# Preparing the state-space tables of a hybrid decoder trunk: real and imaginary parts in one operation, B for two units at once

## The chip, the core and the metric

The kernel runs on one core of a Trainium2 chip. Its time is the device time of one execution in microseconds (us). An execution with the profiler on gives the trace. In the trace PE is the matrix engine (PEld its weight loads), DVE the vector engine, ACT the scalar engine, POOL the GpSimd engine, and SP the engine that issues most DMAs; ACT issues some too. Every engine works through its own list of instructions in order and waits at the first one whose inputs are missing.

## What is computed

Two layers over 16 learned and 512 input positions (528 rows, width 1024). Each layer normalises, projects, runs latent attention (4 heads) and a diagonal state-space mixer (32 groups of 16 channels, 64 complex states each) side by side, adds both, and runs a gated feed-forward of width 2816. The part that matters here is the state-space mixer:

```python
lr = min(a_re, -1e-4); li = a_im; dt = exp(log_dt)[:, None]
mag = exp(lr * dt)
lam_re, lam_im = mag * cos(li * dt), mag * sin(li * dt)
den = lr * lr + li * li
coef_re = ((lam_re - 1) * lr + lam_im * li) / den        # complex (lam - 1) / (lr + i li)
coef_im = (lam_im * lr - (lam_re - 1) * li) / den
bbar_re = coef_re * b_re - coef_im * b_im                # per group, state and channel
bbar_im = coef_re * b_im + coef_im * b_re
# s[t] = lam * s[t-1] + bbar u[t];  y[t] = re(c s[t]) + d * u[t]
```

The kernel runs the recurrence in chunks of 8 positions, and for that prepares matrices from the parameters: powers 0 to 8 of `lam`, rotations of the unit-size `lam` in two tables of six (`lo`, `hi`) whose products give all chunk positions, and per unit of 4 groups the products of these powers with B and C.

## The kernel before, in words

A layer's preparation has a common part, `prep_small` (L389 to L564), on arrays of 128 states by 32 groups: two exponentials (`exp`, L403), sine and cosine, the powers `pw` of `lam` (`cmul`, L466), the coefficients `cc` (L482 to L502), the copies `pf` and `pw` in falling order with signs on ACT (L506 to L510), and the tables `el` and `eh` (`lo`, `hi`, L532 to L562). All of its arithmetic is on DVE (`ON["small"]`), nearly all on 32 elements per partition, real and imaginary parts in separate instructions. Four quarters follow. A quarter builds a table for its 8 groups (`prep_tables`, L566: `tab`, a single buffer, sent to a DRAM tile by SP) and handles two units (`prep_mats`, L597). A unit loads its B and C (`bc`, two buffers, DMA issued by ACT, L602), forms `bbar` in six operations on 64 elements (L609 to L612), `X` on DVE or POOL, transposes `X` on PE into `pt` (L631), copies it by ACT into `Xt` (L633), forms `C` on POOL (L637), multiplies `bbar` with it on PE into `pk` (L643) and copies that by ACT into `K` (L651). `pt`, `pk` and the state-space products share one PSUM buffer (`"one"`).

In layer 0 this runs beside the first projection and attention; `prep_mats` there has its six `bbar` operations on DVE and `C` on POOL. For layer 1 it runs in layer 0's feed-forward phases (`step(nxt, 2, ...)`, L1272), with `bbar`, `X`, `C` and the tables on POOL and `prep_small` again on DVE, between the evacuations of the gate and up products (`g`, `hid`) and the low parts of the weights (`wlo`, L254).

The order on each engine comes from a scheduler that plays the program through with its own durations, with priorities; layer 0's preparation has a raised one (`LATER`). So an edit in `prep_small` can move instructions of anything that runs near it, on any engine. Three points that the change can touch:

- The norm's factor of layer 0 (`factor`, L342): PE sums squares into `nacc` (L352), DVE makes the reciprocal root `nw` in a dozen small instructions (L332 to L336), PE spreads it over rows (`nrb`, L371). Products of the first projection go on without it, but PE works in order and stops at `nrb`.
- Buffers of 128 by 2 by 528 values, `pair` (15 of them): the layer's normalised inputs `x` take eight in layer 0, with half of each unused, since that layer multiplies in plain float32.
- The end of the state-space part: the last unit's `ya` (L760, L761), its store and reload (`yd`, `y`), the gelu `u` on ACT and DVE (L773 to L777), and the gated product (`acc<-u`, the glu) that needs all four `u`.

Of the kernel before, what the change touches and what calls it, by code (L numbers as in the profile page):

```python
# [10 lines left out]
F32 = mybir.dt.float32  # L11
# [15 lines left out]
HC = 16  # L27
# [21 lines left out]
BUFS = (2,4,0,2,1)  # L49
V0 = (1,1)  # L50
# [51 lines left out]
def trunk(ctx: ExitStack, tc: tile.TileContext, A, out, dbg=None):  # L102
# [283 lines left out]
    def small(name):  # L386
        return prep_tile("small", NL, 24, name)

    def prep_small(l):  # L389
# [6 lines left out]
        def rnd(o, x, c):  # L396
            E.tensor_scalar(out=o, in0=x, scalar1=c, scalar2=MAGIC, op0=ALU.mult, op1=ALU.add)
            E.tensor_scalar(out=o, in0=o, scalar1=-MAGIC, scalar2=None, op0=ALU.add)
# [4 lines left out]
        def exp(o, x):  # L403
            n, r, s = small("n"), small("r"), small("s")
            xc = small("xc")
            E.tensor_scalar(out=xc, in0=x, scalar1=-87.0, scalar2=88.0, op0=ALU.max, op1=ALU.min)
            rnd(n, xc, 1.4426950408889634)
            stt(r, n, -0.693359375, xc, ALU.mult, ALU.add)
            stt(r, n, 2.12194440e-4, r, ALU.mult, ALU.add)
            E.tensor_scalar(out=s, in0=r, scalar1=1.0 / 5040, scalar2=None, op0=ALU.mult)  # L410
            for c in (1.0 / 720, 1.0 / 120, 1.0 / 24, 1.0 / 6, 0.5, 1.0):
                stt(s, s, c, r, ALU.add, ALU.mult)
            e = prep_tile("int", NL, 2, "e", I32)
            E.tensor_scalar(out=n, in0=n, scalar1=127.0, scalar2=None, op0=ALU.add)
            V.tensor_copy(e, n)
            V.tensor_single_scalar(out=e, in_=e, scalar=23, op=ALU.logical_shift_left)
            stt(o, s, 1.0, e.bitcast(F32), ALU.add, ALU.mult)
# [8 lines left out]
        k, r, z, s, c = (small(n) for n in ("k", "r", "z", "s", "c"))  # L426
# [21 lines left out]
        cs, sn, t = small("cs"), small("sn"), small("t")  # L448
# [9 lines left out]
        pr, pi = (x.rearrange("p (t g) -> p t g", t=9) for x in (pw[:, 0:9 * NL], pw[:, 9 * NL:18 * NL]))  # L458
        E.memset(pr[:, 0], 1.0)
        E.memset(pi[:, 0], 0.0)  # L460
        mul(E, pr[:, 1], mag, cs)
        mul(E, pi[:, 1], mag, sn)
        tq = prep_tile("tq", 4 * NL, 1)
        tq = tq.rearrange("p (t g) -> p t g", t=4)

        def cmul(re, im, d, n, a0, br, bi):  # L466
            br, bi = (x.unsqueeze(1).to_broadcast([128, n, NL]) for x in (br, bi))
            t1 = tq[:, 0:n]
            dr, di, ar, ai = re[:, d:d + n], im[:, d:d + n], re[:, a0:a0 + n], im[:, a0:a0 + n]
            mul(E, dr, ar, br)  # L470
            mul(E, t1, ai, bi)
            tt(E, dr, dr, t1, ALU.subtract)
            mul(E, di, ar, bi)
            mul(E, t1, ai, br)
            tt(E, di, di, t1, ALU.add)

        cmul(pr, pi, 2, 1, 1, pr[:, 1], pi[:, 1])
        cmul(pr, pi, 3, 2, 1, pr[:, 2], pi[:, 2])
        cmul(pr, pi, 5, 4, 1, pr[:, 4], pi[:, 4])
        yield  # L480

        nr, den, u = small("nr"), small("den"), small("u")  # L482
        CR, CI = small("CR"), small("CI")
        ni = pi[:, 1]
        E.tensor_scalar(out=nr, in0=pr[:, 1], scalar1=-1.0, scalar2=None, op0=ALU.add)
# [4 lines left out]
        mul(E, CR, nr, lr)  # L490
        mul(E, u, ni, li)
        tt(E, CR, CR, u, ALU.add)
        mul(E, CR, CR, den)
        mul(E, CI, ni, lr)
        mul(E, u, nr, li)
        tt(E, CI, CI, u, ALU.subtract)
        mul(E, CI, CI, den)
        cc = prep_tile("cc", 3 * NL, 1)
        CRk, CIn, CIp = (cc[:, i * NL:(i + 1) * NL] for i in range(3))
        V.tensor_copy(CRk, CR)  # L500
        E.tensor_scalar(out=CIn, in0=CI, scalar1=sneg, scalar2=None, op0=ALU.mult)
        E.tensor_scalar(out=CIp, in0=CI, scalar1=spos, scalar2=None, op0=ALU.mult)  # L502
# [15 lines left out]
        def square(dr, di, ar, ai):  # L518
            q = small("q")
            mul(E, q, ai, ai)  # L520
            mul(E, dr, ar, ar)
            tt(E, dr, dr, q, ALU.subtract)
            stt(di, ar, 2.0, ai, ALU.mult, ALU.mult)

        def power2(a, n):
            for i in range(n):
                b2 = small("e0"), small("e1")
                square(*b2, *a)
                a = b2
            return a  # L530

        lo_ = prep_tile("el", 2 * LOW * NL, 1)  # L532
        hi_ = prep_tile("eh", 2 * HIGH * NL, 1)
        lo, hi = ([x.rearrange("p (r t g) -> p r t g", r=2, g=NL)[:, r] for r in range(2)] for x in (lo_, hi_))
        a = power2((cs, sn), 3)
        E.tensor_scalar(out=a[1], in0=a[1], scalar1=sneg, scalar2=None, op0=ALU.mult)
        for x, n in ((lo, LOW), (hi, HIGH)):
            E.memset(x[0][:, 0], 1.0)
            E.memset(x[1][:, 0], 0.0)
            w = 1  # L540
            while w < n:
                if w > 1:
                    a = power2(a, 1)
                V.tensor_copy(x[0][:, w], a[0])
                V.tensor_copy(x[1][:, w], a[1])
                k = min(w, n - w) - 1
                if k:
                    cmul(x[0], x[1], w + 1, k, 1, *a)
                w *= 2
            if x is lo:  # L550

                a = small("e0"), small("e1")
                t = small("q")
                (r2, i2), (r4, i4) = ((x[0][:, w], x[1][:, w]) for w in (2, 4))
                mul(E, a[0], r2, r4)
                mul(E, t, i2, i4)
                tt(E, a[0], a[0], t, ALU.subtract)
                t = small("q")
                mul(E, a[1], r2, i4)
                mul(E, t, i2, r4)  # L560
                tt(E, a[1], a[1], t, ALU.add)
            yield  # L562
        prm["mag8", l] = mag8
# [32 lines left out]

    def prep_mats(l, u, ea, eb):  # L597
# [3 lines left out]
        raw = prep_tile("bc", 448, BUFS[0])  # L601
        nc.scalar.dma_start(raw[:, 0:256], A["ssmbc"][l, u])  # L602
        b1, b2, c1, c2 = (raw[:, i * 64:(i + 1) * 64].rearrange("p (g h) -> p g h", g=4) for i in range(4))

        def bh(ap):
            return ap[:, gs].unsqueeze(2).to_broadcast([128, 4, HC])

        bb1, bb2, t = (raw[:, i * 64:(i + 1) * 64].rearrange("p (g h) -> p g h", g=4) for i in (4, 5, 6))
        for o, x, y, ci in ((bb1, b1, b2, "CIn"), (bb2, b2, b1, "CIp")):  # L609
            mul(ea, o, x, bh(prm["CR"]))  # L610
            mul(ea, t, y, bh(prm[ci]))
            tt(ea, o, o, t, ALU.add)  # L612
# [63 lines left out]
    class Normed:  # L676
# [757 lines left out]
```

## Time and profile before

| | |
|---|---|
| median of 3 runs | 1327.66 us (1321.62 to 1329.62) |
| the profiled execution | 1326.85 us, its span 1325.1 us |
| PE busy | 1273.1 us, 96% of the span |
| DVE, ACT, POOL busy | 793.2, 433.8, 379.2 us |
| layer 0 up to its feed-forward | 0 to some 305 us |
| layer 0's feed-forward, with layer 1's preparation | to some 707 us |

The page of the profile gives busy times, a chain of waits that ended last, and groups of instructions. [...] Instructions of short length overlap in the timeline, so the step from one start to the next says what one costs its engine. A float32 product of 264 columns is one instruction in the program's order and two on PE in the trace.

### The profile page before, as it was taken

Reading aid. Unit: us, or ns where it says so; the run is one execution under the profiler, and the core shown is the slowest. Engines: PE = TensorE matmul, PEld = TensorE weight load, DVE = VectorE, ACT = ScalarE, POOL = GpSimd, SP = SyncE. Lnnn points to the kernel's source line nnn. Section 1 sums busy time; section 2 is a strip of 40 time slices with the busy share of each in tenths; the row PEclk is TensorE's granted clock in tenths of the full one; section 3 lists DMA queues with packets and bytes.
Section 4 is the critical chain, followed back from the end, with each engine's and each line's share of the span. In section 5 each row is a group of like instructions: output and inputs, shape, how many; then the busy total and the mean of one; then the engine's idle time right before and its main releaser. Section 6 shows DMA issues by size and latency. Waiting matters only on the chain.

```text
span 1325.1 us, 20705 instructions
## 1 busy us (share of the span) xinstructions
PE 1273.1 (96%) x8242; PEld 1146.9 (87%) x8242; DVE 793.2 (60%) x1539; ACT 433.8 (33%) x725; POOL 379.2 (29%) x365
## 2 busy tenths in 40 slices
PE   9888999998999999999999999899999999999996
PEld 7677877998999999999999998789788888888885
DVE  8775673577984556357554279765854445445545
ACT  4211444333332232223233226553422222222231
POOL 3544233551174434025304354356200000000001
PEclk9899998999989999999999999999999999999998
DMA  5467543132234444344434536212233332333321
GB/s 196 148 176 185 137 146 93 57 96 68 93 103 140 112 115 104 105 115 114 110 96 124 180 96 217 64 64 65 80 95 86 106 95 92 86 109 95 93 83 64
DMA packets 83728, 145.94 MB, mean 110 GB/s; under 512 B 23472, under 2 KB 51632, under 8 KB 83632
## 3 DMA queue, kind: packets, MB, share of 16 engines
q1 hardware_dynamic: 80032, 141.32, 36.2%
q10 hardware_dynamic: 3600, 3.30, 0.8%
q8 instruction: 65, 1.06, 0.3%
q14 instruction: 31, 0.25, 0.1%
HBM read 121.17 MB, written 23.43 MB: 109 GB/s over the span
## 4 chain that ended last, share of the span: by engine, by line
PE 72%; DVE 9%; ACT 2%; issue 1%; DMA 1%; POOL 1%; DVEq 0%; SPq 0%; ACTq 0%; POOLq 0%
PE da L277 18%; PE ua L277 18%; PE ga L277 17%; PE acc L277 10%; DVE h L197 1%; PE pvo L1103 1%; DVE sq L197 1%; PE acc L265 1%; PE nrb L371 1%; DVE wlo L197 1%; DVE wo L197 1%; PE nacc L352 1%; PE pvo L1106 1%; PE pk L643 1%; DVE x L311 1%
## 5 line engine op out<-in xcount | busy, mean ns | idle before, releaser
L253 ACT CAST whi<-raw 128x1024 fp32r<-128x1024 f32 (+3 forms) x174 | 174.3, 1002 | 536.5 <-issue 145.3
L277 PE MATMUL ga<-x,whi 128*128 128x264 f32 (+1 forms) x1056 | 226.6, 322 | 6.8 <-ACT x L310 4.9
L277 PE MATMUL ua<-x,whi 128*128 128x264 f32 (+1 forms) x1056 | 226.5, 323 | 0.0
L277 PE MATMUL da<-hid,whi 128*128 128x264 f32 (+2 forms) x1088 | 225.3, 316 | 0.3 <-DVE hid L197 0.3
L277 PEld LDWEIGHTS ga<-x,whi 128*128 128x128 f32 x1056 | 163.8, 189 | 25.1 <-ACT x L310 5.6
L197 DVE TENSOR_TENSOR wlo<-raw,whi 128x1024 fp32r<-128x1024 f32 (+1 forms) x130 | 172.3, 1326 | 17.3 <-ACT whi L253 15.1
L277 PEld LDWEIGHTS ua<-x,whi 128*128 128x128 f32 x1056 | 165.9, 191 | 15.9
L277 PEld LDWEIGHTS da<-hid,whi 128*128 128x128 f32 x1088 | 167.3, 188 | 13.9 <-DVE hid L197 0.5
L277 PE MATMUL ua<-x,wlo 128*128 128x264 f32 (+1 forms) x528 | 143.3, 326 | 3.1 <-DVE wlo L197 3.1
L277 PE MATMUL da<-hid,wlo 128*128 128x264 f32 (+2 forms) x544 | 143.7, 317 | 0.3
L277 PE MATMUL ga<-x,wlo 128*128 128x264 f32 (+1 forms) x528 | 142.1, 323 | 0.0
L197 POOL TENSOR_TENSOR wlo<-raw,whi 128x1024 fp32r<-128x1024 f32 (+2 forms) x44 | 95.9, 2180 | 129.6 <-ACT whi L253 129.6
L197 POOL TENSOR_TENSOR o<-h,nr 128x256 f32<-128x256 f32 x8 | 6.1, 797 | 363.8 <-ACT nr L375 363.8
L197 DVE TENSOR_TENSOR h<-da,h 128x528 f32<-128x528 f32 (+2 forms) x50 | 33.9, 677 | 125.8 <-PE da L277 125.8
L277 PEld LDWEIGHTS ua<-x,wlo 128*128 128x128 f32 x528 | 89.1, 191 | 10.7 <-DVE wlo L197 3.3
L277 PEld LDWEIGHTS da<-hid,wlo 128*128 128x128 f32 x544 | 90.2, 188 | 8.6 <-DVE wlo L197 1.3
L197 DVE TENSOR_TENSOR g<-ua,R 128x528 f32<-128x528 f32 (+1 forms) x44 | 30.7, 698 | 110.4 <-PE ua L277 110.3
L277 PEld LDWEIGHTS ga<-x,wlo 128*128 128x128 f32 x528 | 87.9, 189 | 7.7 <-POOL wlo L197 0.4
L265 PE MATMUL acc<-x,raw 128*128 128x264 f32 x320 | 79.5, 408 | 0.0
L197 DVE TENSOR_TENSOR g<-ga,nr 128x528 f32<-128x528 f32 (+1 forms) x44 | 30.7, 698 | 76.7 <-PE ga L277 75.9
L265 PEld LDWEIGHTS acc<-x,raw 128*128 128x128 f32 x320 | 63.8, 203 | 11.9 <-issue 0.5
L197 POOL TENSOR_TENSOR Ct<-bc,pw 128x576 f32<-128x576 f32 x16 | 23.6, 1476 | 112.5 <-PE pk L643 112.5
(291 smaller groups left out, 2182.4 us busy)
## 6 DMA issues: line engine op xcount, KB each, us to landing
raw<-w_gate SPq DMA_DIRECT2D x44, 512.0 KB, 3.6
raw<-w_up SPq DMA_DIRECT2D x44, 512.0 KB, 3.6
raw<-w_down SPq DMA_DIRECT2D x32, 448.0 KB, 3.4
raw<-w_in SPq DMA_DIRECT2D x20, 512.0 KB, 4.2
mat<-mat SPq DMA_DIRECT2D x16, 528.0 KB, 4.1
mt<-k SPq DMA_DIRECT2D x16, 512.0 KB, 4.7
raw<-w_down SPq DMA_DIRECT2D x16, 512.0 KB, 3.5
mat<-tab SPq DMA_DIRECT2D x16, 272.0 KB, 2.7
```

The costliest lines, as they stand in the source:

```text
L197: e.tensor_tensor(out=o, in0=a, in1=b, op=op)
L253: S.copy(hi[:, :n], raw[:, :n])
L265: T.matmul(acc[:, a, 0:hw], w[0][:, off + k * 128:off + (k + 1) * 128], xs[k][:, c0 + a * hw:c0 + (a + 1) * hw], start=k == 0, stop=k == n ...
L277: T.matmul(acc[:, a, 0:hw], wt[:, c], xs[k][:, xi, c0 + a * hw:c0 + (a + 1) * hw], start=j == 0, stop=j == len(terms) - 1)
L311: V.scalar_tensor_tensor(out=lo, in0=src, scalar=scale, in1=hi.bitcast(F32), op0=ALU.mult, op1=ALU.subtract)
L352: T.matmul(acc[:, i:i + 1], x[:, a:a + 128], ones[:, 0:1], start=x is sqs[0], stop=x is sq)
L371: T.matmul(p[:, a - c0:b - c0], y[0:b - a, j:j + 1].to_broadcast([b - a, 128]), ident[0:b - a, 0:b - a], start=True, stop=True)
L643: T.matmul(pk[0:16, g * 128:(g + 1) * 128], bb1[:, g, :], C[:, g * 144 + 16:g * 144 + 144], start=True, stop=True)
L1103: T.matmul(acc[:, a, 0:w], vs[hd // 2, j][0:sn, hd % 2 * 128:hd % 2 * 128 + 128], PT[j][0:sn, 0, c:c + w].bitcast(F32), start=j == 0, stop ...
L1106: T.matmul(acc[:, a, 0:w], vs[hd // 2, j][0:sn, vi, hd % 2 * 128:hd % 2 * 128 + 128], PT[j][0:sn, pi, c:c + w], start=j == 0 and z == 0, s ...
```

## The change

In `prep_small` the real and imaginary parts lie side by side (`two`): a complex product is now two double-width multiplications, the second with the halves read in swapped order, and two half-width additions. The exponential loses two instructions, and the coefficients two. On ACT the eighteen copies in falling order become two that read with a negative step. `prep_inputs` loads B and C of two units at a time, each load as four pieces of 64 values per partition, and forms both units' `bbar` in six operations of 128 elements. In layer 0 these inputs lie in `pair` buffers; the layer's `x` now lie two to a `pair`, which frees four.

```diff
+BCU = 2
-        return prep_tile("small", NL, 24, name)
+        return prep_tile("small", NL, 16, name)
+    def two(name):
+        return prep_tile("two", 2 * NL, 10, name).rearrange("p (r g) -> p r g", r=2)
+    def swapped(x):
+        steps, last = [list(d) for d in x.ap], x[:, 1]
+        steps[1][0] *= -1
+        return bass.AP(last.tensor, last.offset, steps)
...
-            rnd(n, xc, 1.4426950408889634)
+            e = small("e")
+            rnd(n, xc, 1.4426950408889634, MAGIC + 127.0, e)
...
-            E.tensor_scalar(out=n, in0=n, scalar1=127.0, scalar2=None, op0=ALU.add)
-            V.tensor_copy(e, n)
...
-        mul(E, cs, am, c)
-        mul(E, t, b, s)
-        tt(E, cs, cs, t, ALU.subtract)
-        mul(E, sn, am, s)
-        mul(E, t, b, c)
-        tt(E, sn, sn, t, ALU.add)
+        def product2(o, x, re, im, t):
+            n = x.shape[2:-1]
+            mul(E, o, x, both(re, *n))
+            mul(E, t, swapped(x), both(im, *n))
+            tt(E, o[:, 0], o[:, 0], t[:, 0], ALU.subtract)
+            tt(E, o[:, 1], o[:, 1], t[:, 1], ALU.add)
+        lam = two("lam")
+        product2(lam, csn, am, b, two("t"))
...
-        for j in range(9):
-            S.copy(prr[:, j], pr[:, 8 - j])
-            S.activation(pir[:, j], pi[:, 8 - j], AF.Copy, scale=sneg)
+        S.copy(prr, falling(pr))
+        S.activation(pir, falling(pi), AF.Copy, scale=sneg)
...
+    def prep_inputs(l, u, ea):
+        n = BCU * 4
+        if l == 0:
+            raw = pair("bc").rearrange("p a b -> p (a b)")[:, 0:7 * n * HC].bitcast(F32)
+        else:
+            raw = prep_tile("bc", 7 * n * HC, BUFS[0])
+        for i in range(BCU):
+            nc.scalar.dma_start(raw[:, 0:4 * n * HC].rearrange("p (k u x) -> p k u x", k=4, u=BCU)[:, :, i],
+                                A["ssmbc"][l, u + i].rearrange("p (k x) -> p k x", k=4))
...
+        if u % BCU == 0:
+            prep_inputs(l, u, ea)
+        bb1, bb2, c1, c2 = (x[:, u % BCU * 4:u % BCU * 4 + 4] for x in prm["bc"])
...
-                x = pair("x")[:, 0].bitcast(F32)
+                if k % 2 == 0:
+                    self.two = pair("x")
+                x = self.two[:, k % 2].bitcast(F32)
```

DVE has 1542 instructions in the program before and 1440 with the change, ACT 716 and 684, POOL 371 and 347; PE and SP issue as many as before. `prep_small` has, per layer and without what stands between, 173 instructions on DVE before and 134 now, on 6304 and 6144 elements per partition. The order moves on every engine; three places follow.

PE, layer 0's first projection (`acc<-x`), around the factor of the norm. Before:

```order
L265 MATMUL acc<-x,raw 128x264 x48
L352 MATMUL nacc<-cst,sq 128x1 x10
L265 MATMUL acc<-x,raw 128x264 x9
L631 MATMUL pt<-cst,X 128x128 x4
L265 MATMUL acc<-x,raw 128x264 x11
L643 MATMUL pk<-C,bc 16x128 x4
L371 MATMUL nrb<-cst,nw 128x16
```

With the change:

```order
L266 MATMUL acc<-x,raw 128x264 x48
L353 MATMUL nacc<-cst,sq 128x1 x10
L266 MATMUL acc<-x,raw 128x264 x13
L632 MATMUL pt<-cst,X 128x128 x4
L266 MATMUL acc<-x,raw 128x264 x11
L654 MATMUL pk<-C,bc 16x128 x4
L372 MATMUL nrb<-cst,nw 128x16
```

Four more products stand ahead of `nrb`.

ACT, the loads of B and C of the third unit and on (`DMA bc<-ssmbc`), among flips of the tables (`tab<-tab`), copies of `pt` and `pk`, and evacuations of the projection (`cq`, `sq`). Before:

```order
L589 ACTIVATE tab<-tab 128x8x32 [waits DMAHW1_49,DMAHW2_49,DVE_49,Activation_49]
L589 ACTIVATE tab<-tab 128x8x32 [waits DVE_49]
L651 COPY K_644<-pk 16x4x128 [waits DMAHW5_49,DMAHW6_49,DMAHW4_49,DMAHW7_49,PE_49,Pool_49]
L602 DMA bc<-ssmbc 128x256
L589 ACTIVATE tab<-tab 128x8x32 [waits DMAHW0_49,DMAHW7_49,DVE_49,Activation_49]
L589 ACTIVATE tab<-tab 128x8x32 [waits DVE_49]
L633 COPY Xt<-pt 128x512 [waits PE_49]
L651 COPY K_644<-pk 16x4x128 [waits DMAHW3_49,DMAHW4_49,DMAHW2_49,DMAHW5_49,PE_49,Pool_49]
L602 DMA bc<-ssmbc 128x256
```

With the change:

```order
L586 ACTIVATE tab<-tab 128x8x32 [waits DVE_49]
L930 ACTIVATE cq<-acc,gains 128x528 [waits PE_49]
L603 DMA bc<-ssmbc 128x4x64
L603 DMA bc<-ssmbc 128x4x64 [waits DMAHW7_49]
L644 COPY Xt<-pt 128x512 [waits PE_49]
L933 ACTIVATE sq<-acc 128x528
L662 COPY K_575<-pk 16x4x128 [waits DMAHW1_49,DMAHW0_49,DMAHW2_49,PE_49,Pool_49]
L644 COPY Xt<-pt 128x512 [waits DVE_49,PE_49]
```

A load stood behind the copy of a `pk` each time; now both loads of a pair stand ahead of their units' `pt` and `pk`, and all flips of layer 0's four tables stand above this place. The first pair's loads moved the other way: they were ACT's tenth and thirteenth rows, ahead of the first products, and are now behind the flips of `pf` and `pw`.

PE, the end of layer 0's state-space part: the last `ya`, attention's `ptr` and `pvo`, and the glu products `acc<-u`. Before (the first product with the fourth `u`, `u_1857`, stands seven rows below the last one shown):

```order
L761 MATMUL ya<-S,mt 128x66
L1085 MATMUL ptr<-cst,P 128x128 x3
L1103 MATMUL pvo<-PT,v 128x256
L1103 MATMUL pvo<-PT,v 128x272
L1103 MATMUL pvo<-PT,v 128x256 x4
L1085 MATMUL ptr<-cst,P 128x128 x3
L1103 MATMUL pvo<-PT,v 128x256 x2
L265 MATMUL acc<-u_1446,raw 128x264 x2
L265 MATMUL acc<-u_1641,raw 128x264 x2
L265 MATMUL acc<-u_1772,raw 128x264 x2
L1085 MATMUL ptr<-cst,P 128x128
L1103 MATMUL pvo<-PT,v 128x256
```

With the change (the fourth `u` is `u_1759`):

```order
L774 MATMUL ya<-S,mt 128x66
L1116 MATMUL pvo<-PT,v 128x256
L266 MATMUL acc<-u_1674,raw 128x264 x2
L266 MATMUL acc<-u_1348,raw 128x264 x2
L266 MATMUL acc<-u_1543,raw 128x264 x2
L266 MATMUL acc<-u_1674,raw 128x264 x2
L266 MATMUL acc<-u_1348,raw 128x264 x2
L266 MATMUL acc<-u_1543,raw 128x264 x2
L266 MATMUL acc<-u_1674,raw 128x264 x2
L353 MATMUL nacc<-cst,sq 128x1 x5
L266 MATMUL acc<-u_1759,raw 128x264 x6
```

The last `ya` stands later among PE's rows, behind most of attention's work, and the rows left between it and the fourth `u` are fewer.

## Rows read from the trace of the kernel before

**Rows 1.** Busy time by window: engine busy us (instructions), PE's granted clock, DMA share, GB/s.

```profile
350.00:392.00 42.00, 38.93 (x298) 38.71 (x298) 38.44 (x130) 15.11 (x33) 21.41 (x26) 0.92 0.26 77
392.00:707.00 315.00, 314.71 (x2577) 311.05 (x2576) 176.89 (x168) 90.74 (x119) 103.37 (x106) 1.00 0.40 114
```

**Rows 2.** Waits of PE by stretch: who, for whom, us, times, longest.

```profile
PE nrb L371 <- DVE nw L336: 5.6, 1, 5.6
...
PE pk L643 <- ACT Xt L633: 2.3, 1, 2.3
PE nacc L352 <- DVE nr L373: 1.3, 1, 1.3
...
PE acc L265 <- DVE k L197: 1.6, 1, 1.6
...
PE ua L277 <- DVE wlo L197: 3.1, 1, 3.1
```

**Rows 3.** PE alone by window: us, busy, granted clock, DMA share, GB/s.

```profile
48.00:56.00 8.00, 7.23 (x22) 0.58 0.52 166
92.00:96.00 4.00, 4.00 (x13) 0.57 0.38 90
210.00:222.00 12.00, 10.89 (x39) 0.57 0.32 89
```

**Rows 4.** Chain of waits, whole span: start us, us, engine, tile, line, instructions.

```profile
224.10 2.67 PE acc L265 x12
...
338.89 5.86 PE ga L277 x48
...
383.47 8.21 PE ua L277 x44
```

**Rows 5.** Timeline of DVE at the factor: start, us, instruction [idle before <- releaser].

```profile
42.09 0.69 DVE L197 TENSOR_TENSOR X<-bc,pf 128x512 f32<-128x512 f32 x1 [3.77 <-POOL C L197]
...
47.52 1.19 DVE L336 SCALAR_TENSOR_TENSOR nw<-nw 128x5 f32<-128x5 f32 x1
```

**Rows 6.** DMAs issued in 0 to 130 us: KB each, median us to landing.

```profile
mat<-tab SPq DMA_DIRECT2D x8, 272.0 KB, 3.9
...
ud<-u SPq DMA_DIRECT2D x4, 264.0 KB, 5.5
...
bc<-ssmbc ACTq DMA_DIRECT2D x8, 128.0 KB, 4.0
```

**Rows 7.** Waits of DVE, 60 to 130 us.

```profile
DVE bc L197 <- DMA bc<-ssmbc: 13.8, 4, 4.5
DVE tab L197 <- DMA mat<-tab: 4.1, 2, 2.8
```

**Rows 8.** Timeline of DVE in `prep_small`, undisturbed.

```profile
26.54 0.17 DVE L197 TENSOR_TENSOR CI<-CI,den 128x32 f32<-128x32 f32 x1
26.64 0.20 DVE L197 TENSOR_TENSOR bc<-bc,cc 128x64 f32<-128x64 f32 x1
26.78 0.21 DVE L197 TENSOR_TENSOR pw<-pw,tq 128x64 f32<-128x64 f32 x1
```

**Rows 9.** Timeline of DVE late in layer 1's `prep_small`.

```profile
370.09 1.14 DVE L197 TENSOR_TENSOR tq<-el,e 128x32 f32<-128x32 f32 x1
...
376.02 1.45 DVE L197 TENSOR_TENSOR e<-e 128x32 f32<-128x32 f32 x1
...
382.20 1.22 DVE L197 TENSOR_TENSOR wlo<-raw,whi 128x1024 fp32r<-128x1024 f32 x1
```

**Rows 10.** Timeline of ACT: the high part of the same weights.

```profile
373.84 1.05 ACT L253 CAST whi<-raw 128x1024 fp32r<-128x1024 f32 x1 [2.66 <-PE ua L277]
```

**Rows 11.** Timeline of PE: the last of layer 0's `ya`.

```profile
215.84 0.63 PE L761 MATMUL ya<-S,mt 128*128 128x66 f32 x2
```

**Rows 12.** Timeline of DVE: the end of layer 0's last gelu.

```profile
228.25 0.71 DVE L777 SCALAR_TENSOR_TENSOR u<-u,y 128x528 f32<-128x528 f32 x1 [0.71 <-ACT u L776]
```

More of the change, by code (lines that the diff above doesn't have):

```diff
@@ L425, in prep_small @@
         mul(E, th, li, dt)
-        k, r, z, s, c = (small(n) for n in ("k", "r", "z", "s", "c"))
+        k, r, z = (small(n) for n in ("k", "r", "z"))
+        csn = two("csn")
+        c, s = csn[:, 0], csn[:, 1]
         rnd(k, th, 2.0 / math.pi)
@@ L447, in prep_small, with both @@
         E.tensor_scalar(out=am, in0=am, scalar1=-1.0, scalar2=1.0, op0=ALU.mult, op1=ALU.add)
[L448 to L454 removed]
+        def both(ap, *n):
+            return ap.unsqueeze(1).to_broadcast([128, 2, NL]) if not n else ap.unsqueeze(1).unsqueeze(1).to_broadcast([128, 2, *n, NL])
+        def product2(o, x, re, im, t):
[4 more added lines that the diff above has]
+            tt(E, o[:, 1], o[:, 1], t[:, 1], ALU.add)
@@ L480, in prep_small @@
+        cmul(pws, 5, 4, 1, pr[:, 4], pi[:, 4])
         yield
[L482 to L485, printed above, removed]
+        num, den, u, CR = two("num"), small("den"), small("u"), two("CR")
+        E.tensor_scalar(out=num[:, 0], in0=pr[:, 1], scalar1=-1.0, scalar2=None, op0=ALU.add)
+        V.tensor_copy(num[:, 1], pi[:, 1])
         mul(E, den, lr, lr)
@@ L489, in prep_small, with falling @@
         V.reciprocal(out=den, in_=den)
[L490 to L497, printed above, removed]
+        t = two("t")
+        mul(E, CR, num, both(lr))
+        mul(E, t, swapped(num), both(li))
+        tt(E, CR[:, 0], CR[:, 0], t[:, 0], ALU.add)
+        tt(E, CR[:, 1], CR[:, 1], t[:, 1], ALU.subtract)
         cc = prep_tile("cc", 3 * NL, 1)
         CRk, CIn, CIp = (cc[:, i * NL:(i + 1) * NL] for i in range(3))
-        V.tensor_copy(CRk, CR)
-        E.tensor_scalar(out=CIn, in0=CI, scalar1=sneg, scalar2=None, op0=ALU.mult)
-        E.tensor_scalar(out=CIp, in0=CI, scalar1=spos, scalar2=None, op0=ALU.mult)
+        mul(E, CRk, CR[:, 0], den)
+        stt(CIn, CR[:, 1], sneg, den, ALU.mult, ALU.mult)
+        stt(CIp, CR[:, 1], spos, den, ALU.mult, ALU.mult)
         pf = prep_tile("pf", 18 * NL, 1)
         prr, pir = (x.rearrange("p (t g) -> p t g", t=9) for x in (pf[:, 0:9 * NL], pf[:, 9 * NL:18 * NL]))
-        for j in range(9):
-            S.copy(prr[:, j], pr[:, 8 - j])
-            S.activation(pir[:, j], pi[:, 8 - j], AF.Copy, scale=sneg)
+        def falling(x):
+            steps, last = [list(d) for d in x.ap], x[:, 8]
+            steps[1][0] *= -1
+            return bass.AP(last.tensor, last.offset, steps)
+        S.copy(prr, falling(pr))
+        S.activation(pir, falling(pi), AF.Copy, scale=sneg)
         S.activation(pr, prr, AF.Copy, scale=spos)
@@ L543, in prep_small @@
                     a = power2(a, 1)
-                V.tensor_copy(x[0][:, w], a[0])
-                V.tensor_copy(x[1][:, w], a[1])
+                V.tensor_copy(x[:, :, w], a)
                 k = min(w, n - w) - 1
                 if k:
-                    cmul(x[0], x[1], w + 1, k, 1, *a)
+                    cmul(x, w + 1, k, 1, a[:, 0], a[:, 1])
                 w *= 2
             if x is lo:
[L552 to L561, printed above, removed]
+                a = two("e")
+                product2(a, x[:, :, 2], x[:, 0, 4], x[:, 1, 4], two("t"))
             yield
+        lo, hi = ([x[:, r] for r in range(2)] for x in (lo, hi))
         prm["mag8", l] = mag8
```

79 lines of the change are left out of this document (31 added, 48 removed).

## The prediction, made before the change was run

> **What bounds the kernel now.** I read the table by window first, for two stretches that the change touches. After 392 us PE works 314.71 of 315.00 us at its full granted clock, with DVE at 176.89 [rows 1]: nothing shortens that stretch but fewer products, and PE issues as many as before. In 350 to 392 PE has 38.93 of 42.00 us and DVE 38.44, both near full, with PE's clock at 0.92 [rows 1]. So PE is the bound, and the change can only win PE's waits, and the stretches in which PE then runs at half its clock. The list of PE's waits names those that start in the preparation [rows 2]: `nrb` for DVE's `nw` 5.6 us, `pk` for ACT's `Xt` 2.3, `nacc` for `nr` 1.3, `acc` for a DVE evacuation 1.6, and `ua` for DVE's `wlo` 3.1. The clock windows show what follows such a wait: 0.58 after the first, 0.57 near 92 us, 0.57 around the end of layer 0's state-space part [rows 3]. [...] Everything below is counted in PE's time.
>
> The sum is made against the profiled execution, 1326.85 us; the median of the runs shown, 1327.66, is 0.8 above. I take 1% (13.3 us) as what can be told from no change: under 1314.4 is faster, over 1340.9 slower.
>
> **The change, part by part.**
>
> *A. The start of layer 0.* `nrb` waits 5.6 us for `nw`, whose last instruction starts at 47.52 and takes 1.19 [rows 5]. DVE is late there since it first waited 3.77 us for POOL's `C`, until 42.09, to form `X` [rows 5]. The shorter `prep_small` does not move that `X`: in the new order it still waits for POOL. The second quarter's table now stands ahead of `nw` on DVE as well; its single buffer comes free when the first is stored, and such a store lands after 3.9 us [rows 6], so DVE queues there before it reaches the factor. I take `nw` to end where it does now. What is sure is in PE's order: four more products ahead of `nrb`, each two instructions on PE of 2.67/12 = 0.2225 us [rows 4], 8 × 0.2225 = 1.8 us of the wait filled. Ends: 0 if `nw` comes 1.8 later, and the whole wait with the loss at half clock behind it, 5.6 + 7.23 × 0.42 = 8.6 [rows 2, 3]. Taken: 1.8.
>
> *B. Late loads and tables in layer 0.* DVE waits four times for a `bc` load, 13.8 us, the longest 4.5, and twice for the table's buffer, 4.1 [rows 7]. In PE's time this is the 1.3 of `nacc`, the 1.6 of `acc` and the 2.3 of `pk` (its `Xt` is copied by an ACT that stood behind the table) [rows 2], with 4.00 × 0.43 = 1.7 lost at half clock at 92 us [rows 3]: 6.9 in all. Each load stood behind a copy of `pk` on ACT; now a pair of loads stands ahead of both units' `pt` and `pk`, and no flip of a table stands between them. That should end the waits for `bc`. But the pair's `pk` still waits on POOL's `C`, and the tables' waits move up to the factor. I take half, 3.4; ends 0 and 6.9.
>
> *C. The end of layer 0's state-space part.* PE is idle for 12.00 − 10.89 = 1.1 us there and loses 10.89 × 0.43 = 4.7 at half clock [rows 3]. The order differs most here, so I bound it by 5.8 gained and by the 10.0 lost of the slower rival below. I take 0, since the trace has PE at the lower clock there with or without the long wait.
>
> *D. Layer 1's `prep_small`, in the feed-forward.* Here DVE is nearly full and `ua` waits for it. `wlo` starts at 382.20 [rows 9], though `whi`, which it needs, was done at 373.84 + 1.05 = 374.89 [rows 10]: it stood 7.3 us behind `prep_small` in DVE's queue. Undisturbed, the step from one start to the next is 0.10 us for 32 elements and 0.14 for 64 [rows 8]: 0.04 for 32 more elements, 0.00125 each, so 0.06 an instruction is fixed. The change drops 39 instructions and 160 elements: 39 × 0.06 + 160 × 0.00125 = 2.5 us that DVE is earlier, so 2.5 of the 3.1 go. After the wait, 44 products took 8.21 us where at full clock they take 44 × 5.86/48 = 5.37 [rows 4]: 2.8 lost at half clock. Whether a wait of 0.6 still costs the clock no row says; I take half, 1.4. D = 2.5 + 1.4 = 3.9. Ends: 0, since some small instructions late in `prep_small` take 1.14 or 1.45 in place of 0.17 [rows 9] and a few of these hide the whole gain; and 3.1 + 2.8 = 5.9.
>
> [...]
>
> *Edits without a price.* ACT has 32 instructions fewer in all and POOL 24: ACT is busy 15.11 of 42.00 us and 90.74 of 315.00 in the windows of layer 1's preparation [rows 1], and no wait of PE but `pk`'s 2.3 names ACT [rows 2]. The price of this cover going is at most that 2.3, counted in B. The longer `bbar` operations (128 elements for 64) halve their count and are in the 102 instructions that DVE loses. The `x` two to a buffer adds no instruction.
>
> Sum: 1.8 + 3.4 + 0 + 3.9 = 9.1; 1326.85 − 9.1 = 1317.75, **1318 us**.
>
> **The rivals.**
>
> *Faster: the waits go whole.* If the early loads let the preparation run ahead, B gives 6.9, C 5.8, D 5.9, and A its 1.8: 20.4, 1306 us. For it: DVE's 13.8 us of waiting for `bc` [rows 7] is more than PE's waits that follow. Against: `X` waits on POOL [rows 5], which no edit speeds up in layer 0.
>
> *Slower: the last glu waits for the last gelu.* Now the last `ya` ends at 215.84 + 0.63 = 216.47 [rows 11] and the last `u` at 228.25 + 0.71 = 228.96 [rows 12], 12.5 us later; PE fills them with attention. In the new order little attention is left behind the last `ya`: one `pvo`, 14 products (28 × 0.2225 = 6.2 us [rows 4]) and five `nacc`, an estimate of 7.7 us with the short ones. Then PE waits 12.5 − 7.7 = 4.8, and if the next 12 us run at 0.57 as they do now [rows 3], that is 12 × 0.43 = 5.2 more: 10.0. What A and B won is then waited away, since the state-space chain sets this place, and D stays: 1326.85 − 3.9 + 10.0 = 1333 us. It decides if the last `ya` is not at least 4.8 us earlier than now. Without D it is 1337. For it: the rows in PE's order. Against: the scheduler put attention ahead because the chain was expected later, and PE's work ahead of the last `ya` is then larger.
>
> *No change.* The gains of A and B come back as other waits, and D is hidden by slow small instructions [rows 9]: 1325, give or take 2.
>
> *The first load late.* The first pair's loads now stand behind `pf` and `pw` on ACT, and a load takes 4.0 us to land [rows 6]; DVE's `prep_small` is at 26.78 in the powers and the coefficients [rows 8], a few us before `bbar`. I take 1.0 to 2.5 us of lateness, which goes on to `X` and `nw`: A becomes −1.5 and the sum 5.8, 1321 us. [...]
>
> **How the numbers follow.** Forecast 0.40 (1313 to 1323), faster rival 0.25 (1300 to 1313), slower rival 0.14 (1328 to 1340), no change 0.12, first load late 0.09. The range from 1304 to 1336 leaves out about a third of the faster rival and of the slower one, and holds 0.82. Under 1314.4 lie the faster rival and the edge of the forecast: 0.30. Over 1340.9 lies only what the slower rival may cost beyond its price: 0.06. Within 1%: 0.64.
>
> **What would show it.** A: the wait at `nrb` about 3.8 and `nw` ending near 48.7. B: no wait of DVE for `bc` after the first pair, and the clock near 92 us at 1.00. C: the granted clock around the last `ya`, and whether a wait stands before the product with the fourth `u`. D: the wait of `ua` for `wlo` under 1 us, and steps of 0.10 to 0.14 between `prep_small`'s starts. The prediction is wrong if `nw` moves by more than 2 us, if PE waits for the fourth `u`, or if a new wait of DVE for `tab` or of ACT for a load stands in the place of those removed.

## The result, and the profile after

The changed kernel takes 1332.99 us (median of 17 runs, 1327.92 to 1338.38) where the kernel before takes 1326.70 on the same chip (17 runs): a ratio of 1.0054, 95% interval 1.0038 to 1.0070, so 6 us slower by the medians and 7 by the ratio, where 9 us faster was forecast. The profiled execution took 1338.38 us, its span is 1335.9, 10.8 more than before; it is the longest of the 17, so its rows say where time stands, while sizes come from the medians. The page's line on the engines:

```profile
PE 1279.0 (96%) x8242; PEld 1151.7 (86%) x8242; DVE 788.7 (59%) x1437; ACT 428.9 (32%) x693; POOL 365.3 (27%) x341
```

DVE, ACT and POOL do less than before and PE is busy 5.9 us longer for the same 8242 instructions, at a mean granted clock of 0.977 for 0.980. PE alone by window (us, busy, granted clock, DMA share, GB/s), first after, then before:

```profile
30.00:60.00 30.00, 25.65 (x116) 0.89 0.44 135
60.00:110.00 50.00, 42.08 (x206) 0.93 0.68 173
110.00:150.00 40.00, 35.55 (x177) 0.96 0.63 148
205.00:245.00 40.00, 38.23 (x210) 0.96 0.37 115
300.00:320.00 20.00, 15.87 (x91) 0.74 0.17 52
```

```profile
30.00:60.00 30.00, 24.21 (x104) 0.83 0.41 127
60.00:110.00 50.00, 46.47 (x236) 0.97 0.74 188
110.00:150.00 40.00, 35.73 (x195) 1.00 0.58 138
205.00:245.00 40.00, 37.56 (x179) 0.87 0.26 74
300.00:320.00 20.00, 16.12 (x119) 0.91 0.26 79
```

Between 60 and 110 us PE works 4.4 us less than before and at a lower clock; at the end of the state-space part (205 to 245) it is better than before, and at the start of the feed-forward (300 to 320) its clock is lower. To see what lasts, I cut PE's timeline of every kernel, those of the experiments below included, at the same products: the first `ga` of layer 0's feed-forward, its first `da`, the first `ga` of its second part, its last `da`, the first `ga` of layer 1's feed-forward, and the last `da` of all (us, differences of start times, one execution each):

```
                    to ga   ga-da  da-ga  ga-da  da-ga  ga-last da
before             295.22   96.66  41.72  272.35 229.78 373.94
after              296.20   99.17  46.01  272.77 230.10 376.69
layer 0 only       298.29   96.43  41.95  272.84 229.91 376.56
layer 1 only       294.39   97.01  45.15  272.33 233.00 373.94
prep_small only    291.56   95.89  45.33  272.42 230.15 376.85
inputs only        291.75   95.57  44.54  272.76 228.71 375.14
flips on POOL      293.98   95.91  41.92  272.77 226.36 375.12
coefficients last  294.14   93.78  49.21  272.25 230.06 376.72
both of these      295.89   93.61  44.95  273.41 228.80 375.09
before, flips      299.45   95.90  41.72  272.40 231.70 373.97
before, -350       294.90   96.44  42.77  272.33 230.50 377.35
before, -400       294.41   93.78  44.26  272.47 226.92 376.91
early loads        290.17   99.16  46.28  272.95 226.99 375.27
early, flips       292.03   99.16  41.96  272.94 232.80 376.21
early, flips again 287.26   99.30  41.97  272.95 230.03 372.95
 with coefs between 289.48  95.99  41.94  272.99 225.82 375.69
 old prep_small    288.20   97.99  41.96  272.95 228.76 372.95
 old in layer 1    291.26   96.88  41.96  272.98 232.31 372.97
```

The fourth column is PE's bare work and nearly the same for all. The first shows how far one order strays from run to run: before's order (before, layer 1 only, before with flips) has 294.4 to 299.5, the changed one (after, layer 0 only, flips on POOL, coefficients last, both) 294.0 to 298.3. So three things are left. Layer 0 gained nothing. The third column is 3 to 5 us longer in every kernel with new code in layer 1 and ACT's flips (7.5 with the coefficients last), and 2.5 to 3 longer in two others. The last column is 1 to 3 longer in most that differ from before in layer 0; but one kernel that was traced twice (`early, flips` and `again`) has 376.21 and 372.95 there, at a granted clock of 0.83 and 1.00 between 940 and 960 us, so one execution does not fix that column.

**Layer 0.** PE's timeline after (start, us, instruction, idle before and its releaser):

```profile
42.47 1.12 PE L642 MATMUL pt<-cst,X 128*128 128x128 f32 x4 [3.78 <-DVE X L198]
...
50.47 1.03 PE L372 MATMUL nrb<-cst,nw 16*128 16x16 f32 x6
...
72.27 0.63 PE L642 MATMUL pt<-cst,X 128*128 128x128 f32 x4 [2.46 <-DVE nw L358]
...
79.22 1.08 PE L372 MATMUL nrb<-cst,nw 16*128 16x16 f32 x5 [2.98 <-DVE nw L337]
```

The wait of 5.6 us at `nrb` [rows 2] is gone, and one of 3.78 for `X` stands 8 us ahead of it: 1.8 saved. This is the first unit's `X`, and DVE makes it 6 us later than before. Before, then after:

```profile
35.52 0.67 DVE L197 TENSOR_TENSOR X<-X,Xt 128x512 f32<-128x512 f32 x1
```

```profile
41.73 0.68 DVE L198 TENSOR_TENSOR X<-X,Xt 128x512 f32<-128x512 f32 x1
```

The first pair's loads are issued at 27.63 us where the first unit's load was issued at 5.38, and the order on DVE has `bbar` at 35.34 where it was at 26.27; DVE does not wait for the load itself. Then two new waits follow. The timelines of ACT and DVE, execution of after, show why:

```profile
60.91 0.42 ACT L586 ACTIVATE tab<-tab 128x256 f32<-128x256 f32 x1 [4.17 <-DVE tab L198]
61.23 0.55 ACTq L603 DMA_DIRECT2D bc<-ssmbc  x1
...
59.20 1.25 DVE L198 TENSOR_TENSOR tab<-eh,el 128x288 f32<-128x288 f32 x2 [2.51 <-DMA mat<-tab]
...
67.65 0.79 DVE L198 TENSOR_TENSOR bc<-bc,cc 128x128 f32<-128x128 f32 x3 [3.31 <-DMA bc<-ssmbc]
...
72.23 1.45 DVE L333 TENSOR_SCALAR nw<-nw 128x5 int32<-128x5 int32 x1
73.72 2.32 DVE L198 TENSOR_TENSOR nw<-nw 128x5 f32<-128x5 f32 x1
```

All four tables stand up front. DVE's last one waits 2.51 us for the single buffer's store, ACT's flip waits for DVE, the second pair's load is behind the flip and issued at 61.23, DVE waits 3.31 for it, and the third `X` and behind it the second factor `nw` come late (DVE waits another 4.65 for the third pair's load, at 96.10); with POOL's `C` and `X` beside it (72.26 to 77.4) two instructions of `nw` took 1.45 and 2.32 us, where those from 77.42 on, with POOL idle, took 0.16 or 0.17.

**Layer 1, near 376 us.** Timeline after of ACT, DVE and PE:

```profile
366.26 1.05 ACT L254 CAST whi<-raw 128x1024 fp32r<-128x1024 f32 x1 [0.63 <-PE ua L278]
...
368.91 1.18 DVE L198 TENSOR_TENSOR el<-el,e 128x64 f32<-128x64 f32 x1
...
372.36 2.65 DVE L198 TENSOR_TENSOR el<-el,tq 128x32 f32<-128x32 f32 x2
...
375.04 1.21 DVE L198 TENSOR_TENSOR wlo<-raw,whi 128x1024 fp32r<-128x1024 f32 x1
...
376.30 0.51 PE L278 MATMUL ua<-x,wlo 128*128 128x264 f32 x2 [3.48 <-DVE wlo L198]
```

`whi` was ready at 367.31, `wlo` came 7.7 us later (7.3 before), and PE waits 3.48 (3.1 before [rows 2]). Two instructions on 32 elements take 2.65 us, with POOL's `X` and `C` beside them (372.35 to 374.96), where two undisturbed ones, at 378.35, take 0.28.

**Layer 1, near 400 us**, a place that the prediction does not name:

```profile
397.70 0.43 ACT L586 ACTIVATE tab<-tab 128x256 f32<-128x256 f32 x1 [4.78 <-POOL tab L198]
398.46 0.43 ACT L586 ACTIVATE tab<-tab 128x256 f32<-128x256 f32 x1 [0.34 <-POOL tab L198]
398.80 0.93 ACT L254 CAST whi<-raw 128x896 fp32r<-128x896 f32 x1
...
399.76 1.40 DVE L198 TENSOR_TENSOR wlo<-raw,whi 128x896 fp32r<-128x896 f32 x1 [3.84 <-ACT whi L254]
401.08 1.60 DVE L198 TENSOR_TENSOR g<-g 128x528 f32<-128x528 f32 x1
...
402.72 0.63 ACT L308 CAST hid<-g 128x528 fp32r<-128x528 f32 x1 [2.52 <-DVE g L198]
...
403.41 0.63 PE L278 MATMUL da<-hid,whi 128*128 128x264 f32 x3 [1.32 <-ACT hid L308]
```

ACT waits 4.78 us for POOL's second table with the cast `whi` behind the flips; `wlo`, `g` and `hid` follow late, PE waits 0.68 and 1.32 and runs at half clock for some 4 us behind (granted 0.50 to 0.52 from 404 to 407 us). Before, the second table's flips stood behind this `hid`, and PE had no wait between 390 and 415 us. ACT's timeline before:

```profile
395.47 0.64 ACT L307 CAST hid<-g 128x528 fp32r<-128x528 f32 x1 [2.52 <-DVE g L197]
399.67 0.43 ACT L589 ACTIVATE tab<-tab 128x256 f32<-128x256 f32 x1 [3.56 <-POOL tab L197]
```

### The profile page after: what moved, and what is told of

Same layout as the page of the kernel before. It is cut to its first block, busy times and chain, and to the rows that moved or that the text cites. A ratio compares the mean times of both kernels' runs of the same rounds, so it can differ in the third digit from the quotient of the medians.

```text
span 1335.9 us, 20541 instructions
## 1 busy us (share of the span) xinstructions
PE 1279.0 (96%) x8242; PEld 1151.7 (86%) x8242; DVE 788.7 (59%) x1437; ACT 428.9 (32%) x693; POOL 365.3 (27%) x341
## 4 chain that ended last, share of the span: by engine, by line
PE 74%; DVE 15%; DMA 5%; ACT 2%; issue 2%; POOL 2%; SPq 0%; DVEq 0%; ACTq 0%; POOLq 0%
PE da L278 18%; PE ua L278 18%; PE ga L278 17%; PE acc L278 10%; PE acc L266 2%; DVE sq L198 1%; DVE h L198 1%; PE nrb L372 1%; DMA bc<-ssmbc 1%; DMA mat<-tab 1%; PE pvo L1116 1%; PE pvo L1119 1%; DVE wlo L198 1%; DMA yd<-ys 1%; PE pk L654 1%
## 5 line engine op out<-in xcount | busy, mean ns | idle before, releaser
L198 POOL TENSOR_TENSOR o<-h,nr 128x256 f32<-128x256 f32 x8 | 6.1, 797 | 363.6 <-ACT nr L376 363.6
```

What stands on the lines that cost most here:

```text
L198: e.tensor_tensor(out=o, in0=a, in1=b, op=op)
```

## The experiments

All were timed in five rounds against before. Theory 1: layer 0's gains come back as waits and the loss is made in the feed-forward beside layer 1's preparation. Theory 2, its rival: the loss comes from layer 0's new order through the clock at the feed-forward's start. Later ones are named where they come.

**One layer at a time.** The new code in one layer (`prep_small`, pairs of loads, and for layer 0 the `x` two to a buffer), the old in the other.

```diff
-        yield from prep_small(l)
+        yield from (prep_small if NEW[l] else prep_small_old)(l)
+NEW, BC, XP = (1, 0), (2, 1), 1     # layer 0 alone: new prep_small, units to a load, x two to a buffer
+NEW, BC, XP = (0, 1), (1, 2), 0     # layer 1 alone
```

> The change in layer 0 alone (its prep_small, its pairs of loads, the x two to a buffer); layer 1 prepares as before. Theory 1 (the loss is made in the feed-forward, where layer 1 is prepared beside it; layer 0's gains only come back as other waits): 0 to +2 us against before, the first product of the feed-forward (ga) at about 296. Theory 2 (the loss comes from layer 0's new order, by a longer half-clock stretch where the feed-forward's norm begins): +4 to +7 us, and the granted clock between 305 and 316 us as low as with the whole change.

> The change in layer 1 alone; layer 0 stands as before, instruction for instruction. Theory 1: +4 to +7 us against before; PE still waits 3 us or more for wlo near 380, and a new wait for hid and wlo stands near 400. Theory 2: within 2 us of before.

Layer 0 alone: 1330.13, ratio 1.0032 [1.0015, 1.0049]. Layer 1 alone: 1330.17, 1.0046 [1.0024, 1.0067]. Each layer costs something by itself (theory 1 had allowed layer 0 up to 2 us), so neither theory is whole; and the two add to more than the whole change costs. Layer 1 alone has the wait for `hid` and the third column at 45.15; layer 0 alone has neither, but 376.56 in the last column.

**One half of the change.** Only the merged `prep_small` and copies, then only the inputs of two units.

```diff
+NEW, BC, XP = (1, 1), (1, 1), 0
+NEW, BC, XP = (0, 0), (2, 2), 1
```

> Both layers with the new prep_small and the two copies in falling order, but B and C loaded and formed one unit at a time and x one to a buffer as before. Theory 1, if POOL's wide bbar is what slows DVE: -3 to +1 us against before, DVE's small instructions near 365 to 375 at 0.2 us again. Theory 1, if it is any POOL work beside prep_small: +2 to +6, since the shorter prep_small only releases POOL earlier. Theory 2 says nothing certain: the order of layer 0 is a third one.

> Only the inputs of two units at once and x two to a buffer; prep_small as before. If the wide bbar on POOL is what costs: +3 to +7 us against before, with more of DVE's small instructions over 0.4 us. If it is the shorter prep_small that starts POOL earlier: -2 to +2.

1330.35, ratio 1.0048 [1.0024, 1.0073], and 1328.23, 1.0020 [1.0000, 1.0040]. The first half costs; the second's interval starts at no change, so it may cost nothing. Both have the third column over 44; it is not the wide `bbar` alone. With the inputs alone the order near 400 us is that of before (the flips ahead of `hid` are the first table's), but PE comes to its first `da` at 387.3 where before it came at 391.9, the flips are only 1.9 us earlier, and PE waits 1.2 us for `hid`: time won ahead of this place is partly waited away at it.

**Layer 1's flips and coefficients.** The flips go to POOL; then, with the flips on ACT, the coefficients and falling copies are written after `el` and `eh`; then both.

```diff
-            S.activation(o[:, :, 0:BACK], flip, AF.Copy, scale=-1.0 if x else 1.0)
+            P.tensor_scalar(out=o[:, :, 0:BACK], in0=flip, scalar1=-1.0 if x else 1.0, ...)   # layer 1
...
+        if l == 1:
+            yield from coefs()        # now behind the loop that makes el and eh
```

> The whole change, with layer 1's table flips done by POOL in place of ACT; PE and DVE keep the changed kernel's order, row for row. Theory 1a (near 400 us ACT's flips wait for POOL's tables and hold the casts whi behind them, so wlo, the gate value g and hid come late): PE's waits for hid and wlo near 400 go, with the half-clock stretch behind them: 3 to 4.5 us less than the changed kernel, +3 to +4 against before. Rival 1b (DVE is slow there only because POOL works beside it): the waits stay or grow with POOL's added work: +7 to +9 against before.

1330.20, ratio 1.0022 [0.9998, 1.0045]: 1a's price, with an interval that touches before. PE's waits between 390 and 415 us are gone and the third column is 41.92. ACT's timeline there: the cast waits for PE and no longer for a table.

```profile
389.53 0.95 ACT L257 CAST whi<-raw 128x896 fp32r<-128x896 f32 x1 [4.26 <-PE ua L281]
...
392.25 0.63 ACT L311 CAST hid<-g 128x528 fp32r<-128x528 f32 x1 [1.29 <-DVE g L201]
```

> The whole change, with layer 1's coefficients and its copies in falling order after the tables el and eh, so that POOL's bbar, X and C can't start beside DVE's small instructions. If POOL's work slows these (0.4 to 1.3 us in place of 0.2): the small instructions stay at 0.2 us, PE's wait of 3.5 us for wlo near 376 falls under 1, and the time is 3 to 5 us less than the changed kernel, +2 to +4 against before. If DVE's queue is long whatever POOL does: the wait stays over 2.5 and the time within 2 us of the changed kernel.

1332.79, ratio 1.0042 [1.0019, 1.0066]. The wait for `wlo` is gone (second column 93.78 for 99.17), and the time is the changed kernel's, where 3 to 5 us less was expected: the gain is given back at the next place, where `hid` now stands right behind a flip that waits 7.11 us for POOL.

```profile
395.97 0.42 ACT L777 ACTIVATE tab<-tab 128x256 f32<-128x256 f32 x1 [7.11 <-POOL tab L201]
396.30 0.61 ACT L311 CAST hid<-g 128x528 fp32r<-128x528 f32 x1
...
396.96 0.87 PE L281 MATMUL da<-hid,whi 128*128 128x264 f32 x5 [2.91 <-ACT hid L311]
```

> The whole change with both: layer 1's flips on POOL and its coefficients after the tables. If both reasons hold and add up: 6 to 8 us less than the changed kernel, -1 to +1 against before, with what is left at layer 0 and at the start of layer 1's feed-forward. If one only moves the other's wait: +3 to +5.

1331.28, ratio 1.0042 [1.0016, 1.0069], a miss: without the flips in the way, `X` is the late one, since POOL starts later (its `bbar` at 375.97 us with the coefficients last, at 360.20 in after).

```profile
402.09 0.66 PE L842 MATMUL pt<-cst,X 128*128 128x128 f32 x4 [3.39 <-POOL X L201]
```

**Another order of the kernel before.** Theory 3: an order other than the picked one costs by itself.

```diff
-LATER = (-300,300)
+LATER = (-350,300)      # and -400
```

> The kernel before with another priority for layer 0's preparation (-350 for -300): the same instructions in another order. Theory 3 (any other order costs, since the order before is a picked one): +3 to +6 us. If order alone matters little: within 2 us of before.

> The kernel before with priority -400 for layer 0's preparation: the same instructions in a third order. Theory 3 (an order other than the picked one costs): +3 to +7 us, of it some 3 at the start of layer 1's feed-forward, as at -350. If -350 was bad luck: within 2 us.

1332.64, ratio 1.0045 [1.0024, 1.0067], and 1329.62, 1.0025 [1.0012, 1.0039]. The same instructions in two other orders are slower by 6 and 3 us. Both have some 377 in the last column, as the changed kernel has, and -400 has the third column at 44.26 too, with a wait of 1.2 us for `hid` (there too PE comes sooner, at 388.2, behind the first table's flips). PE's waits from 905 to 970 us at -350:

```profile
PE ga L277 <- DVE x L311: 2.2, 1, 2.2
```

and after:

```profile
PE ga L278 <- ACT x L311: 2.4, 1, 2.4
```

Before, the longest one there is 1.3 us. Layer 0's order carries through the scheduler to layer 1's output projection, where the sums `h` and the inputs `x` are taken in another sequence. A wait of this size does not settle the cost, though: `early, flips again` has one of 2.2 us at this place, no half clock behind it (granted 1.00 from 940 to 960 us), and a last column 1 us shorter than before's. So these runs show that an order costs 3 to 6 us, and not at which place.

**The control for the flips**: the kernel before with layer 1's flips on POOL, the same edit as above.

> The kernel before with layer 1's flips on POOL alone, as a control; PE and DVE keep their order, row for row. In before no flip holds up a cast that PE waits for near 400 us, so theory 1a expects within 2 us of before; if moving the flips helps any order (ACT freed), -2 to -4.

1324.23, ratio 0.9988 [0.9964, 1.0011]: no difference that can be told. In this order, where `hid` stands ahead of the second table's flips, the flips cost nothing that shows.

**Layer 0's loads together.** All four pairs are issued behind the falling copies.

```diff
+                for u in (0, 2, 4, 6):
+                    raw = prm["raw", 0, u] = pair("bc")...        # prep_inputs takes it from here
+                    for i in range(2):
+                        nc.scalar.dma_start(raw[...][:, :, i], A["ssmbc"][0, u + i]...)
```

> The whole change, with all eight of layer 0's loads of B and C issued together, behind the copies in falling order and ahead of the tables' flips (the x two to a buffer leave room for them); only the first 60 us of the order differ from the changed kernel's. Theory 4 (layer 0's gain went because the second pair's loads stand behind the last flips, which wait for tables and their stores, so that DVE waits for bc and the next X and the second factor come late): DVE's waits for bc go, PE's waits between 50 and 110 us fall by 4 us or more, the first product of the feed-forward stands 4 to 6 us earlier than in the changed kernel, and the time is +1 to +4 against before. Rival: the tables themselves, all four up front, make X and the factor late: the first product moves by under 2 us.

1327.03, ratio 1.0004 [0.9987, 1.0022], some 6 us less than the changed kernel and a little better than expected. The first column falls from 296 (the mean of the five with the changed order, 294.0 to 298.3) to 290 (the mean of the five with these loads and the new layer 0, 287.3 to 292.0). That is theory 4's size and not its rival's.

> The same, and layer 1's flips on POOL. If both reasons hold and add: -2 to +1 against before. If either gives its gain back: +2 to +4.

With the flips' edit besides: 1319.73 (7 runs), ratio 0.9945 [0.9925, 0.9965]: both reasons add up, and by more than expected. PE keeps the order of the kernel with the early loads alone, row for row. It was repeated as the reference of the last batch:

> Both repairs once more, on the same chip as the three others, as their reference: 5 to 8 us under before, and near 1320.

1323.95 (12 runs), ratio 0.9984 [0.9965, 1.0003], short of the 5 us expected; the two intervals touch at 0.9965. Taken together by their runs the two are 0.3% under before, 4 us, so the first set was probably a lucky one. PE's waits of the second up to 145 us, the longest, but for one ahead of the first product:

```profile
PE pt L839 <- DVE X L202: 5.8, 1, 5.8
PE nacc L357 <- DVE nr L378: 3.6, 1, 3.6
PE sc L1262 <- DVE q L202: 1.7, 1, 1.7
...
PE nrb L376 <- DVE nw L341: 1.3, 1, 1.3
```

Among DVE's longer waits there, none is for `bc`; it now waits 13.3 us, in two pieces, for POOL's `C`. PE stops for the first `X` and for a copy `nr`.

**POOL beside DVE, with PE's order held.** Both repairs, and layer 1's coefficients and falling copies between `el` and `eh`.

```diff
                 product2(a, x[:, :, 2], x[:, 0, 4], x[:, 1, 4], two("t"))     # the last step of el
+                if l == 1:
+                    yield from coefs()
```

> Both repairs (layer 0's loads together, layer 1's flips on POOL), and layer 1's coefficients between the tables el and eh; PE keeps the order of early4_flips, row for row. If POOL's work beside prep_small makes wlo late at 372 us: about half of DVE's slow small instructions go, the wait of 3.5 us falls under 1.5 and the time is 2 to 4 us less than early4_flips. If the wait only moves to hid or to pt near 400 us, as it did with the coefficients last: within 1.5 us of early4_flips, or slower.

1321.71, ratio 0.9962 [0.9941, 0.9984], 2 us less than its reference with intervals that overlap; the second column is 95.99 for 99.30. The wait of 3.5 us for `wlo` is gone, and so is the half clock behind it (granted 0.50 from 369 to 371 us in the reference, 1.00 throughout from 340 to 380 here). The instructions on `el` (ns: shortest, median, longest; first and last start) in the reference, and here:

```profile
L202 DVE TENSOR_TENSOR el<-el,tq x4: 179/740/1430, 363.6 to 369.7; 128x32 f32<-128x32 f32 x4
```

```profile
L202 DVE TENSOR_TENSOR el<-el,tq x4: 186/190/193, 357.8 to 358.8; 128x32 f32<-128x32 f32 x4
```

PE's waits for `wlo` from 296 to 420 us in the reference:

```profile
PE ua L282 <- DVE wlo L202: 3.5, 1, 3.5
```

and all of PE's waits there here:

```profile
PE ga L282 <- ACT x L315: 3.6, 1, 3.6
PE pt L847 <- POOL X L202: 1.9, 1, 1.9
PE ga L282 <- DVE x L316: 0.5, 1, 0.5
```

No wait for `wlo` is left, in the same order of PE. The order on DVE differs, but not in favour of `wlo`: between the gate product and this `wlo` stand 14 small instructions in the reference, which take 9.9 us with the evacuation of `ua` among them, and 21 here, which take 3.7 us with the same evacuation and a wait of 0.6. So the wait's cause is shown; what it is worth in time is not, since the intervals overlap.

**Is the merged `prep_small` worth anything?** Both repairs with the old one in both layers, and in layer 1 alone (`NEW` as in the first experiment).

```diff
-NEW = (1, 1)
+NEW = (0, 0)      # then (1, 0)
```

> Both repairs with the prep_small of before in both layers: real and imaginary parts in separate instructions. If the merged prep_small has a worth once the repairs are made: 3 to 6 us slower than early4_flips (its 39 instructions a layer, 2.5 us each time where they are on the path). If the gain is all of the loads and the flips: within 2 us of early4_flips.

> The same with the prep_small of before in layer 1 alone. If the merged one gains nothing there because POOL, released earlier, slows DVE by as much: within 1 us of early4_flips, PE's wait for wlo 3.0 to 3.5 either way. If it gains as predicted: 2 to 4 us slower.

1321.65, ratio 0.9968 [0.9951, 0.9985], and 1324.50, 0.9980 [0.9961, 0.9998]. Neither can be told from the reference. So the loads and the flips carry the gain, and 39 instructions fewer a layer have no worth that these runs can show.

## Why the prediction was wrong, point by point

- **The base** held: PE is the bound, and nothing after 410 us of layer 0's feed-forward moved (fourth column).
- **A, 1.8 us**: the size came (5.6 to 3.78 us), the mechanism only in part. The factor `nw` ended at 49.5 us for 48.7, as forecast. But PE stops for the first unit's `X`, 8 us ahead of `nrb`, and that `X` is 6 us later; A followed the second unit's `X` and did not ask about the first. That the difference is 1.8 is luck.
- **B, 3.4 us, is the step that failed in layer 0.** It read that a pair of loads stands ahead of its own `pt` and `pk`, and not that it stands behind the last flips, which wait for DVE, which waits for a store. PE's waits from 50 to 145 us (`pt`, `nrb`, `sc`, `pk`, and so on) are some 13 us in the profile, some 8 before. Shown: with the loads early the first product of the feed-forward moves 5 to 6 us ahead. The forecast's own sign that it would be wrong, a wait for `tab` or a load in the place of those removed, is what came.
- **C, 0**: the half clock around the last `ya` [rows 3] is gone in the profile of after (granted 1.00 from 215 to 235 us), and PE's window 205 to 245 gained 0.7 us busy at 0.96 for 0.87. But before's order ran with it and without it (before with the flips has 0.50 from 214 to 226 us, layer 1 alone no half clock there), so this is not the change's. The slower rival's wait before the fourth `u`, the other sign of being wrong, came as 1.51 us, not 4.8. That this rival's time, 1333, is the measured one is chance: its mechanism carries little of it. The row of PE after:

```profile
236.58 8.19 PE L266 MATMUL acc<-u,raw 128*128 128x264 f32 x28 [1.51 <-DVE u L790]
```

- **D, 3.9 us, failed too.** The 39 instructions are gone, but POOL starts its `bbar`, `X` and `C` when the coefficients are there, and beside them DVE's small instructions take 0.4 to 1.4 us. The low end, 0, named this [rows 9] and should have been taken: `wlo` waits on the instructions that run beside POOL, not on all of them. Shown by the coefficients between the tables, with PE's order held. In the changed kernel `wlo` came no earlier behind `whi` than before (7.7 us for 7.3). Undisturbed, 32 and 64 elements took 0.17 and 0.20 us [rows 8]; the disturbed ones, at up to 1.4, decide here.
- **"Edits without a price": the flips on ACT, put at nothing, cost 3 to 5 us near 400 us.** In the kernels with the new `prep_small` in layer 1 the order sets ACT's flips of the second table ahead of `hid`; that the scheduler does so because `prep_small` looks shorter to it is likely, not shown. POOL's tables come no earlier: the first starts at 384.01 for 384.77 before. That ACT is idle most of the time was the argument for a price of nothing; here one wait of 4.78 us at the head of its queue held `whi` behind it, in an engine that is busy 32% of the span. And that no wait of PE but the 2.3 us of `pk` names ACT holds for the first 145 us alone: at the feed-forward's start PE waits 3.6 us for ACT's `x`, before and after. Shown by the flips on POOL, with and without the early loads, and by the control.
- **Missed: the price of another order.** The prediction never asked what a new order costs far from the edit. Two other orders of the unchanged kernel cost 3 to 6 us, shown by -350 and -400. That 1 to 3 of it lies at layer 1's feed-forward is what single executions suggest; there the same kernel spreads by 3.3, and where this part of the loss is made stays open.
- **First load late** (a rival at 0.09): right in kind, for two pairs. The first pair's loads are issued 22 us later, DVE forms that `bbar` 9 us later, and PE waits for that `X`; the second pair's are held by the flips. Its size, A at -1.5, does not follow from its own 1.0 to 2.5 us of lateness, by which A is 0.8 to -0.7. The loads in pieces of 256 bytes landed after 4.9 us, in pieces of 1,024 after 4.0 [rows 6]; but they are also issued closer together (0.69 us apart at 27.63, where the first two were 1.49 apart), and no run changes the size of the pieces alone, so what the smaller pieces cost is not shown. What delayed `bc` was the issue, not these 0.9 us. The row of the DMAs in 0 to 130 us after (KB each, median us to landing):

```profile
bc<-ssmbc ACTq DMA_DIRECT2D x8, 128.0 KB, 4.9
```

- **The sum**: layer 0 gave 0 for 5.2, layer 1's stall 0 for 3.9, and two unseen costs took 3 to 5 and some 1 to 3, against a loss of 6 to 7 us. How these add up within a run can't be closed better than the 2 us of the intervals.

## What to carry to other kernels

A shorter producer is worth something only if its consumers' queues are not set by something else: after each removed wait, name the head of every in-order queue behind it and what that head waits for. Look for work that a faster step releases beside itself, and price the instructions that run beside it by the disturbed rows (here a median of 740 ns for 190). A load that moves down its queue moves everything that the scheduler places behind it, even where nobody ends up waiting for the load itself (here 22 us for the first pair's loads, and 9 for the `bbar` made from them). Where a scheduler sets the order, time two other orders of the unchanged kernel first: here they alone cost 3 to 6 us, as much as the edit, and an edit's own worth shows only after its misplaced loads and copies are put right.

## What the runs showed of the hardware

Most of the spread of one kernel goes with its clock. In 331 executions the time of a kernel falls by 0.9 us for each 0.001 of its mean granted clock, and this goes with 74% of the variance within a kernel; before ran between 0.973 (1336 us) and 0.987 (1320 to 1323 us). Which of the two causes the other is not shown: the clock also falls behind waits of PE. At one mean clock, 0.980, the changed kernel is 5.6 us slower than before, and the kernel with the two repairs 5.0 and 3.7 us faster in its two sets, so the order of these results does not rest on it.

The half-clock stretch behind the wait of 3.6 us at the feed-forward's start lasts some 4 us in before and some 10 in after (granted clock 0.91 and 0.74 between 300 and 320 us), and again some 4 with the flips on POOL (second column 95.91 for after's 99.17), whose PE and DVE rows are the same as after's: what decided its length I did not find.

A small instruction of DVE that runs beside POOL's work took up to 1.4 us where it took 0.2 without it: the four on `el` had a median of 740 ns in the reference of the last batch, where POOL works from 351.4 to 368.4 us and the first two of them start at 363.6, and of 190 with the coefficients between the tables, where POOL starts at 363.7, behind all four.
